# A hybrid encoder layer on one core: the first stage's order written by hand, with convolution steps between the state-space transposes, and the first two feed-forward weights split in front of the product before them

## The chip, the cores and the metric

The kernel runs on one core of one Trainium2 chip. A core has five engines with queues of their own, which meet only through semaphores: TensorE (PE in the profile; PEld is its weight load), VectorE (DVE), ScalarE (ACT), GpSimd (POOL) and SyncE (SP). [...] The metric is the device time of one execution in microseconds, as a median over runs. Lower is better.

## The reference

One encoder layer over 512 rows of width 1024, in float32. Cut to what is computed:

```python
h = rms_norm(x, norm_mix_g);  p = h @ w_in          # q|k|v (512 each) | conv input (512) | u (256)
o_sb   = stick_breaking_attention(q, k, v)          # 8 heads x 64, causal, q and k normalised
o_conv = conformer_conv(p[..., s3:s4], ...)         # gate, causal depthwise conv (31 taps), LayerNorm, swish, product
o_ssm  = s5_ssm(p[..., s4:], ...)                   # 16 groups x 16 channels, 64 complex states each
x = x + concat(rms_norm(o_sb), rms_norm(o_conv), rms_norm(o_ssm)) @ w_out
x = x + memory_cross_attention(rms_norm(x), rms_norm(mem), ...)   # 4 heads x 256, 256 memory rows
gate, up = split(rms_norm(x) @ ffn_w_in)            # hidden 2816
x = x + (silu(gate) * up) @ ffn_w_out
```

and, of the state-space branch, whose coefficients stand in the change:

```python
dt = exp(log_dt);  mag = exp(lr * dt)
ar, ai = mag * cos(li * dt), mag * sin(li * dt)
fr, fi = ((ar - 1) * lr + ai * li) / den, (ai * lr - (ar - 1) * li) / den     # den = lr*lr + li*li
bbr, bbi = fr * br - fi * bi, fr * bi + fi * br
```

## The kernel before, in words

**Products.** Each float32 operand is split into a high part (a cast to fp32r) and a low part (the rest). `mm3` (L112) makes a product of three matmuls, high x high and the two mixed ones, so L114, L115 and L116 are nearly all matmuls of the profile. A weight is loaded by `load_k` (L104) and `load_w` (L89): a DMA from SP into a staging buffer of the ring `wst` (3 buffers), a cast on ACT into `whi`, a subtraction on DVE into `wlo` (rings of 4). Where DVE is to be spared, ACT writes the negative of the high part into the low buffer, and a DMA from POOL adds the weight to it. A buffer of a ring is given out again when all that reads it is done.

**Order.** The program is written as generators. A planner places instructions on each engine by their place in the program and by when their inputs should be there; `yield` numbers tell `weave` (L187) how much PE time of side work to put in between. Inside `manual_schedule(engines=...)` the instructions of the named engines keep the order in which they are written; instructions from outside still slip in between them.

**The first stage** (L893 to L1024). The 512 rows of x come in four blocks (`squares`, `scale`, `turn`, `low`, L936 to L966: sum of squares on ACT, normalisation on DVE, 8 transposes on PE with casts on ACT, low parts on DVE). Beside it runs `ssm` (L287), the state-space branch S5, stepped by `aside` (L928) and `next(S5)`:

- L303 to L349: `dt`, the eight angles `th` (seven multiplications, L307), sine and cosine as polynomials on DVE; two Exp on ACT, `mag` and `r4` (L322, L323).
- L361 to L378: the table E on POOL, by doubling.
- L381 to L424: some 33 operations on eight columns and six on 128 (`apr`, `api`, `fr`, `fi`, `bb`) on DVE.
- L428 to L437: the product u (96 matmuls of 256 columns), copied by ACT to `uT`; L439 to L451: eight transposes of `uT` into `uk`, DVE copies, eight more into `UT`, ACT copies.
- L455 to L485: `wr`, `wi`, `Qr`, `Qi` (`products`) on DVE, and their transposes `wT`; L489 to L502: the products `kp`, copied to `Kf` on ACT, finished on DVE (L501); from L505 the products S, the scans V (L524), X, y, then the gated output and its norm (to L581).

In the block of L974 the orders of DVE, ACT and POOL are by hand, PE's isn't. It ends with the first `next(S5)` behind the E memsets, which builds E. The second `next(S5)` (L1007), from L381 through `UT`, stands outside. Then `weave` runs S5 with side work: `conv_gemm` (L584: 96 matmuls of 512 columns in eight steps, weights wc0 to wc3; its gating, L605 and L606, makes `hp`), then the attention projections `sb_proj(0)` and `sb_proj(1)` (L669), each step with three of the 62 convolution taps (L617) on DVE. The attention stage opens its memory only when S5 is done (L1018).

**The start of the feed-forward stage** (L1335 to L1373). The last cross-attention product xo has four row blocks t, each 8 x 3 matmuls of 512 columns with the weights wx10 to wx13 (`wo_rows`, L1185). Behind each block come the residual and norm (`wo_norm`, `wo_scale`), 8 transposes (`hf_turn`) and splits (`hf_split`). The FFN's first product is done by a scheme of seven half-size products (units of weights a and b, `unit_raw` L1246; sums of them `unit_tsum`, `unit_t`; sums of the rows T1 to T4). The first two units' weights a are split by `unit_a_queue` (L1266), with ACT casts into `whi` and `wlo` and an adding DMA from POOL. In this block PE, DVE, ACT and POOL all follow the written order.

Of the kernel before, what the change touches and what calls it, by code (L numbers as in the profile page):

```python
# [11 lines left out]
F32 = mybir.dt.float32  # L12
F32R = mybir.dt.float32r
# [59 lines left out]
def layer(ctx: ExitStack, tc: tile.TileContext, A: dict, out: bass.AP, dbg=None):  # L73
# [35 lines left out]
    def cols(parts, c):  # L109
        return [x[:, c] for x in parts]  # L110
# [176 lines left out]
    def ssm(sp, sk, wu):  # L287
# [17 lines left out]
        yield 0  # L305
        for k in range(1, NA):
            v.tensor_scalar(th[:, k, :], th[:, 0, :], float(LC * 2 ** (k - 1)), None, op0=ALU.mult)  # L307
            yield 0
# [12 lines left out]
        yield 0  # L321
        s.activation(mag, lrdt, AF.Exp)  # L322
        s.activation(r4, lrdt, AF.Exp, scale=float(LC))  # L323

# [23 lines left out]
        yield 0  # L348
        v.tensor_scalar(cs, x2, -2.0, 1.0, op0=ALU.mult, op1=ALU.add)  # L349
        yield 0  # L350

# [14 lines left out]
        for k in range(7):  # L366
# [10 lines left out]
            for x in {3: (wr, wi), 5: (Kf,)}.get(k, ()):  # L377
                g.memset(x, 0.0)  # L378
        yield 2

        apr = small("apr", LC + 1, NST)  # L381
# [42 lines left out]
        v.tensor_tensor(bb[:, 1], b1, b2, op=ALU.add)  # L424
        yield 0


        uT = sp.tile([P, 2, LC, NCH], F32, tag="uT", name="uT")  # L428
        pu = [ps("acc", f"u{ct}") for ct in range(2)]
        for h in range(2):  # L430
            c = slice(h * 256, h * 256 + 256)
            for ct in range(2):
                for k in range(KD):
                    o = (k % 4) * 256 + ct * P
                    mm3(pu[ct][:, c], cols(wu[k // 4], slice(o, o + P)), [x[:, k, c] for x in xn], k == 0, k == KD - 1)
        for ct in range(2):
            s.copy(uT[:, ct].rearrange("p j c -> p c j"), pu[ct].rearrange("p (c j) -> p c j", j=LC))  # L437

        uk = sp.tile([P, NST, LC, 32], F32, tag="wTr", name="uk")  # L439
        UT = sp.tile([P, NST, NCH], F32, tag="UT", name="UT")  # L440
        for ct in range(2):
            pt = ps("tp", f"uk{ct}")
            for j in range(LC):
                te.transpose(pt[:, j * P:(j + 1) * P], uT[:, ct, j, :], ident)
            v.tensor_copy(uk[:, ct * 4:ct * 4 + 4], pt.rearrange("p (j t h) -> p t j h", j=LC, h=32))
        for hf in range(2):
            pt = ps("tp", f"UT{hf}")
            for k in range(4):
                T = hf * 4 + k
                te.transpose(pt[:, k * P:(k + 1) * P], uk[:, T].rearrange("p j h -> p (j h)"), ident)  # L450
            s.copy(UT[:, hf * 4:hf * 4 + 4, :].rearrange("p t c -> p (t c)"), pt)  # L451

        yield SSM_FILL[0]
# [129 lines left out]

    def conv_gemm():  # L584
        order = (2, 0, 3, 1)
        pa = {n: ps("acc", f"cv{n}") for n in order}

        def step(n, k, b):
            o = (k % 2) * 512 + n * P
            mm3(pa[n], cols(b, slice(o, o + P)), [x[:, k, :] for x in xn], k == 0, k == KD - 1)  # L590

        for kc in range(2):
            b = load_k(A["w_cv"], 2 * kc, 512, f"wc{kc}")
            for k in (2 * kc, 2 * kc + 1):
                for n in order:
                    step(n, k, b)
                yield 2600
        b = [load_k(A["w_cv"], 2 * kc, 512, f"wc{kc}") for kc in (2, 3)]
        for n in order:
            for k in range(4, KD):  # L600
                step(n, k, b[k // 2 - 2])
            if n < 2:
                with tc.high_priority(offset=EV_CONV):
                    sg = cvp.tile([P, SEQ], F32, tag="csg", name=f"csg{n}")
                    sigmoid(sg, pa[2 + n])  # L605
                    v.tensor_tensor(hp[:, n, CPAD:], pa[n], sg, op=ALU.mult)  # L606
            yield 2600
# [285 lines left out]
    with tc.tile_pool(name="ssmp", bufs=1, side="right") as sp:  # L893
# [80 lines left out]
        with tc.manual_schedule(engines={v.engine, s.engine, g.engine}):  # L974
            for b in range(3):
                for x in vzs[b]:
                    g.memset(x[:, :, 1, :].bitcast(F32), 0.0)
            aside(18)
            squares(0)
            aside(2)  # L980
            scale(0)
            squares(1)
            turn(0)
            aside(2)
            u_high(0)
            scale(1)
            low(0)
            turn(1)
            squares(2)
            aside(99)  # L990
            g.memset(hp[:, :, :CPAD], 0.0)
            g.memset(tmpm, -2.0 ** 100)
            g.affine_select(out=tmpm, in_=tmpm, pattern=[[1, P]], compare_op=ALU.is_ge, fill=0.0, base=0, channel_multiplier=-1)
            u_low(0)
            low(1)
            u_high(1)
            squares(3)
            scale(2)
            turn(2)
            u_low(1)  # L1000
            scale(3)
            turn(3)
            low(2)
            low(3)
            next(S5)
        dbg("xn", xn)
        next(S5)  # L1007
        mxc = [slotB("mxc" + i, F32R, i, 1) for i in "hl"]
# [4 lines left out]
        T = conv_taps()  # L1013
        side = chain(conv_gemm(), along(sb_proj(0), T, 3), along(sb_proj(1), T, 3))
        weave(S5, side)
# [152 lines left out]
    with tc.tile_pool(name="ff", bufs=1, side="right") as ff:  # L1168
# [15 lines left out]

        def wo_rows(t):  # L1185
            acc = ps("acc", f"xo1{t}")
            for k in range(KD):
                mm3(acc, [x[:, k % 4, t * P:(t + 1) * P] for x in oT[k // 4]], cols(wo1[k // 2], slice((k % 2) * 512, (k % 2) * 512 + 512)),
                    k == 0, k == KD - 1)
            return acc  # L1190

# [73 lines left out]

        def unit_a_queue(p, x, a, b, w):  # L1266

            h, l = [wp.tile([P, 2, 512], F32R, tag="w" + part, bufs=WB, name=f"wa{p}{x}{part}") for part in ("hi", "lo")]
            s.copy(h, a)
            s.activation(l, h, AF.Copy, scale=-1.0)  # L1270
            g.dma_start(l.rearrange("p j n -> p (j n)"), A["w_gu"][p, x, 0], accum_op=ALU.add)  # L1271
            w["11"], w["12"] = [(h[:, i], l[:, i]) for i in range(2)]
# [63 lines left out]
        ws = {i: unit_raw(*units[i], v) for i in range(2)}  # L1336
        outs, pts = {}, {}
        with tc.manual_schedule(engines={te.engine, v.engine, s.engine, g.engine}):
            for t in range(NT):
                acc = wo_rows(t)  # L1340
                if t > 0:
                    hf_turn(t - 1)
                if t == NT - 1:
                    unit_a_queue(*units[1], *ws[1])
                wo_norm(t, acc)
                if t == NT - 1:
                    hf_diff(t - 1)
                    unit_tsum(*units[0], *ws[0], v)
                wo_scale(t)
                if t == NT - 2:  # L1350
                    unit_a_queue(*units[0], *ws[0])
                if t > 0:
                    hf_split(t - 1)
# [117 lines left out]
```

## Time and profile before

| | us |
|---|---|
| median of 3 runs | 821.97 (818.88 to 825.33) |
| profiled execution | 821.17 |
| its span in the trace | 819.5 |

The span runs from the first instruction to the last; 1.7 us of the execution lie around it. A row of a timeline has the start, the length, the engine, the line, the operation with output <- input, the shape and the count, and, in brackets, how long the engine stood idle before it and what ended that. Rows of matmuls overlap: the distance from one start to the next is the rate. "Granted clock" is the share of full speed that TensorE's clock had in a stretch.

### The profile page before, as it was taken

What the parts mean: (1) busy time and instruction counts of PE and PEld (TensorE: products, weight loads), DVE (VectorE), ACT (ScalarE), POOL (GpSimd) and SP (SyncE); (2) the same over time, 40 slices, a digit from 0 to 9 for tenths busy, and PEclk for the clock granted to TensorE, in tenths of its full rate; (3) what the DMA queues carried; (4) which work ended last, traced back from release to release, by engine and by line L of the source; (5) the groups of instructions that cost most, each with busy time, mean ns of one, the idle gap of its engine ahead of it and who ended that gap; (6) DMA issues with size and microseconds to landing.
All of it is one profiled execution on the core that took longest, in us unless ns stands there. A gap on an engine that the chain in (4) does not pass through costs nothing.

```text
span 819.5 us, 12228 instructions
## 1 busy us (share of the span) xinstructions
PE 783.1 (96%) x4640; PEld 685.2 (84%) x4640; DVE 623.6 (76%) x1079; ACT 415.4 (51%) x771; POOL 180.5 (22%) x155
## 2 busy tenths in 40 slices
PE   5799999999999999999999789999999999999998
PEld 3678999887776778888888789999999999888886
DVE  8979989677998958466847699899999997333333
ACT  6345385997878837355624654344444442322320
POOL 4910011000000000000000006676666761000000
PEclk9979999998999999999999999999999999999999
DMA  6232578525122323320451422333333322232222
GB/s 221 72 84 58 117 156 179 122 84 181 33 94 87 104 83 117 109 78 26 129 154 52 78 81 100 104 104 103 105 113 121 121 85 71 84 103 81 99 78 102
DMA packets 25116, 83.42 MB, mean 102 GB/s; under 512 B 3041, under 2 KB 3297, under 8 KB 25058
## 3 DMA queue, kind: packets, MB, share of 16 engines
q1 hardware_dynamic: 22466, 75.31, 28.9%
q0 software_dynamic: 2592, 7.34, 5.8%
q8 instruction: 36, 0.59, 0.3%
q14 instruction: 22, 0.18, 0.1%
HBM read 80.54 MB, written 2.10 MB: 101 GB/s over the span
## 4 chain that ended last, share of the span: by engine, by line
PE 83%; DVE 10%; ACT 2%; issue 2%; DMA 1%; POOL 0%; POOLq 0%; DVEq 0%
PE fo L115 5%; PE fo L114 5%; PE fo L116 5%; PE f L116 2%; PE f L115 2%; PE f L114 2%; PE qkv L114 2%; PE qkv L116 2%; PE qkv L115 2%; PE xo L114 2%; PE xo L115 2%; PE xo L116 2%; PE xq L114 2%; PE xq L116 2%; PE xq L115 2%
## 5 line engine op out<-in xcount | busy, mean ns | idle before, releaser
L617 DVE SCALAR_TENSOR_TENSOR cac<-hp,pk,cac 128x512 f32<-128x512 f32 x60 | 42.3, 742 | 0.0
L1251 POOL TENSOR_TENSOR wgb<-wgb 128x512 f32<-128x512 f32 x18 | 33.0, 1831 | 40.2 <-DMA wgb<-in_w_gu_dram 30.1
L1276 POOL TENSOR_TENSOR wga<-wga 128x512 f32<-128x512 f32 x20 | 27.3, 1363 | 41.3 <-DVE wga L1275 41.3
L1252 POOL TENSOR_TENSOR wgb<-wga,wgb 128x512 f32<-128x512 f32 x18 | 36.0, 2002 | 0.3
L1271 POOL DMA_DIRECT2D wa00lo<-in_w_gu_dram x1 | 0.9, 880 | 159.9 <-ACT wa00lo L1270 159.9
L1324 POOL TENSOR_TENSOR aF<-aF,fup 128x1024 f32<-128x1024 f32 x10 | 34.2, 3420 | 6.2 <-DVE fup L1320 5.2
L735 DVE TENSOR_TENSOR_SCAN ss<-sa,ss 128x512 f32<-128x512 f32 (+3 forms) x32 | 27.0, 859 | 2.5 <-ACT sa L731 1.9
L774 POOL TENSOR_TENSOR sqa<-sqa,sq 128x512 f32<-128x512 f32 x3 | 3.9, 1288 | 88.5 <-ACT sq L773 88.5
L1275 DVE TENSOR_TENSOR wga<-wgb,wga 128x512 f32<-128x512 f32 x22 | 22.9, 1039 | 0.0
L120 ACT CAST wTh<-wT 128x384 fp32r<-128x384 f32 (+2 forms) x40 | 14.8, 378 | 8.3 <-PE wT L750 7.0
L121 DVE TENSOR_TENSOR wTl<-wT,wTh 128x384 fp32r<-128x384 f32 (+2 forms) x40 | 16.2, 412 | 3.4 <-ACT wTh L120 3.3
L720 PE MATMUL z<-kh,qh 64*128 64x512 f32 (+3 forms) x32 | 13.2, 413 | 2.0 <-DVE ss L737 1.9
L728 ACT ACTIVATE sa<-z 128x384 f32<-128x384 f32 (+1 forms) x24 | 12.8, 532 | 4.7 <-PE z L723 4.4
L720 PEld LDWEIGHTS z<-kh,qh 64*128 64x128 f32 x32 | 6.0, 186 | 10.3 <-DVE ss L737 3.8
L737 DVE TENSOR_TENSOR ss<-z,ss 128x384 f32<-128x384 f32 (+1 forms) x24 | 14.3, 595 | 0.2
L738 ACT ACTIVATE ss<-ss 128x384 f32<-128x384 f32 (+1 forms) x24 | 13.6, 565 | 0.5 <-DVE ss L737 0.3
L730 ACT ACTIVATE sa<-sa 128x384 f32<-128x384 f32 (+1 forms) x24 | 13.8, 573 | 0.1
L731 ACT ACTIVATE sa<-sa 128x384 f32<-128x384 f32 (+1 forms) x24 | 13.7, 569 | 0.1
L750 PE MATMUL wT<-ident,ss 128*128 128x128 f32 x80 | 13.1, 284 | 0.2 <-DVE ql L124 0.2
L813 DVE SCALAR_TENSOR_TENSOR xr<-wo,rb,xr 128x512 f32<-128x512 f32 x16 | 11.9, 747 | 1.8 <-PE wo L116 1.4
L1322 ACT ACTIVATE aF<-aF 128x1024 f32<-128x1024 f32 x11 | 11.6, 1055 | 2.9 <-DVE aF L1320 1.8
L729 ACT ACTIVATE ss<-z 128x384 f32<-128x384 f32 (+1 forms) x24 | 12.8, 535 | 0.1
(2207 smaller groups left out, 3256.2 us busy)
## 6 DMA issues: line engine op xcount, KB each, us to landing
wgb<-in_w_gu_dram SPq DMA_DIRECT2D x22, 512.0 KB, 3.3
wga<-in_w_gu_dram SPq DMA_DIRECT2D x22, 512.0 KB, 3.4
for<-in_w_fo_dram SPq DMA_DIRECT2D x22, 512.0 KB, 3.3
xr<-in_x_dram SPq DMA_DIRECT2D x4, 512.0 KB, 5.0
out_dram<-xr SPq DMA_DIRECT2D x8, 256.0 KB, 2.0
xbh<-in_x_dram SPq DMA_DIRECT2D x2, 512.0 KB, 4.9
xbl<-in_x_dram SPq DMA_DIRECT2D x2, 512.0 KB, 7.7
mt<-in_mem_dram SPq DMA_DIRECT2D x2, 512.0 KB, 3.9
```

Source lines behind the costliest of these rows:

```text
L114: te.matmul(o, a[0], b[0], start=start, stop=False)
L115: te.matmul(o, a[0], b[1], start=False, stop=False)
L116: te.matmul(o, a[1], b[0], start=False, stop=stop)
L121: v.tensor_tensor(lo, src, hi, op=ALU.subtract)
L617: v.scalar_tensor_tensor(a, x, w, a, op0=ALU.mult, op1=ALU.add)
L720: te.matmul(zo, q[0], k[0], start=True, stop=False)
L735: v.tensor_tensor_scan(ts[:, c][:, ::-1], ta[:, c][:, ::-1], ts[:, c][:, ::-1], 0.0, op0=ALU.add, op1=ALU.add)
L1251: eng.tensor_tensor(b[:, 0], b[:, 1], b[:, 2], op=ALU.add)
L1252: eng.tensor_tensor(b[:, 1], a[:, 0], b[:, 1], op=ALU.subtract)
L1275: v.tensor_tensor(a[:, 0], b[:, 0], a[:, 0], op=ALU.subtract)
L1276: eng.tensor_tensor(a[:, 1], a[:, 1], a[:, 0], op=ALU.subtract)
L1324: (g if i + 1 < len(units) else v).tensor_tensor(aF[p], aF[p], dst, op=ALU.mult)
```

## The change

In the first stage:

- `th`: the seven multiplications become four, by doubling, on 1, 1, 2 and 3 columns of eight.
- the two Exp `mag` and `r4` move from in front of the polynomials to behind them.
- in `ssm`, the product u with its copies, and the transposes with theirs, move in front of the coefficients (L381 to L424), with three new yields (3, 4, 5).
- `conv_gemm` gets its weights from outside; wc0 and wc1 are loaded in the first hand-ordered block, behind the last `low`; that block now also holds u.
- a second hand-ordered block (PE, DVE, ACT) follows: twelve conv matmuls, the `uk` transposes, the load of wc2, twelve conv matmuls, the `UT` transposes, the load of wc3, two times twelve conv matmuls, the coefficients, the products with the `wT` transposes. The other half of the conv product stays side work.
- POOL's memsets of `hp` and `tmpm` and its select come first; the `aside` counts change.

At the start of the feed-forward stage:

- `wo_rows` takes a list of k: first k 0 and 1 of all four row blocks, then k 2 to 7 block by block.
- `unit_a_queue` of unit 1 comes in front of all, with its parts in a `wst` and the `fup` buffer; that of unit 0 comes between the two passes.

```diff
-        for k in range(1, NA):
-            v.tensor_scalar(th[:, k, :], th[:, 0, :], float(LC * 2 ** (k - 1)), None, op0=ALU.mult)
+        for k0, k1, c in ((1, 0, LC), (2, 1, 2), (3, 1, 4), (5, 1, 16)):
+            n = {1: 1, 2: 1, 3: 2, 5: 3}[k0]
+            v.tensor_scalar(th[:, k0:k0 + n, :], th[:, k1:k1 + n, :], float(c), None, op0=ALU.mult)
             yield 0
...
-        s.activation(mag, lrdt, AF.Exp)
-        s.activation(r4, lrdt, AF.Exp, scale=float(LC))
...
         v.tensor_scalar(cs, x2, -2.0, 1.0, op0=ALU.mult, op1=ALU.add)
+        s.activation(mag, lrdt, AF.Exp)
+        s.activation(r4, lrdt, AF.Exp, scale=float(LC))
         yield 0
...
         yield 2
 
+        uT = sp.tile([P, 2, LC, NCH], F32, tag="uT", name="uT")
...
+            s.copy(uT[:, ct].rearrange("p j c -> p c j"), pu[ct].rearrange("p (c j) -> p c j", j=LC))
+        yield 3
...
+            v.tensor_copy(uk[:, ct * 4:ct * 4 + 4], pt.rearrange("p (j t h) -> p t j h", j=LC, h=32))
+        yield 4
...
+            s.copy(UT[:, hf * 4:hf * 4 + 4, :].rearrange("p t c -> p (t c)"), pt)
+
+        yield 5
+
         apr = small("apr", LC + 1, NST)
...
         for kc in range(2):
-            b = load_k(A["w_cv"], 2 * kc, 512, f"wc{kc}")
+            b = first[kc]
...
-        b = [load_k(A["w_cv"], 2 * kc, 512, f"wc{kc}") for kc in (2, 3)]
+        b = first[2:]
...
+            g.memset(hp[:, :, :CPAD], 0.0)
+            g.memset(tmpm, -2.0 ** 100)
+            g.affine_select(out=tmpm, in_=tmpm, pattern=[[1, P]], compare_op=ALU.is_ge, fill=0.0, base=0, channel_multiplier=-1)
             aside(18)
             squares(0)
-            aside(2)
             scale(0)
             squares(1)
+            aside(6)
             turn(0)
-            aside(2)
             u_high(0)
             scale(1)
+            aside(99)
             low(0)
             turn(1)
             squares(2)
-            aside(99)
...
             low(3)
+            wc = [load_k(A["w_cv"], 2 * kc, 512, f"wc{kc}") for kc in range(2)]
             next(S5)
+            next(S5)
+        CV = conv_gemm(wc)
+        with tc.manual_schedule(engines={te.engine, v.engine, s.engine}):
+            for i in range(2):
+                next(CV)
+                next(S5)
+                wc.append(load_k(A["w_cv"], 4 + 2 * i, 512, f"wc{2 + i}"))
+            for _ in range(2):
+                next(CV)
+            for _ in range(2):
+                next(S5)
...
-        def wo_rows(t):
-            acc = ps("acc", f"xo1{t}")
-            for k in range(KD):
+        def wo_rows(t, ks):
+            if ks[0] == 0:
+                xo[t] = ps("acc", f"xo1{t}")
+            for k in ks:
...
+            if spare:
+                h = wp.tile([P, 2, 512], F32R, tag="wst", bufs=3, name=f"wa{p}{x}hi")
+                l = ff.tile([P, 2, 512], F32R, tag="fup", bufs=1, name=f"wa{p}{x}lo")
...
+            unit_a_queue(*units[1], *ws[1], spare=True)
             for t in range(NT):
-                acc = wo_rows(t)
+                wo_rows(t, (0, 1))
+            unit_a_queue(*units[0], *ws[0])
+            for t in range(NT):
+                acc = wo_rows(t, range(2, KD))
                 if t > 0:
                     hf_turn(t - 1)
-                if t == NT - 1:
-                    unit_a_queue(*units[1], *ws[1])
                 wo_norm(t, acc)
...
                 wo_scale(t)
-                if t == NT - 2:
-                    unit_a_queue(*units[0], *ws[0])
                 if t > 0:
                     hf_split(t - 1)
```

More of the change, by code (lines that the diff above doesn't have):

```diff
@@ L379, in ssm @@
         yield 2
+        uT = sp.tile([P, 2, LC, NCH], F32, tag="uT", name="uT")
+        pu = [ps("acc", f"u{ct}") for ct in range(2)]
+        for h in range(2):
+            c = slice(h * 256, h * 256 + 256)
+            for ct in range(2):
+                for k in range(KD):
+                    o = (k % 4) * 256 + ct * P
+                    mm3(pu[ct][:, c], cols(wu[k // 4], slice(o, o + P)), [x[:, k, c] for x in xn], k == 0, k == KD - 1)
+        for ct in range(2):
+            s.copy(uT[:, ct].rearrange("p j c -> p c j"), pu[ct].rearrange("p (c j) -> p c j", j=LC))
+        yield 3
+        uk = sp.tile([P, NST, LC, 32], F32, tag="wTr", name="uk")
+        UT = sp.tile([P, NST, NCH], F32, tag="UT", name="UT")
+        for ct in range(2):
+            pt = ps("tp", f"uk{ct}")
+            for j in range(LC):
+                te.transpose(pt[:, j * P:(j + 1) * P], uT[:, ct, j, :], ident)
+            v.tensor_copy(uk[:, ct * 4:ct * 4 + 4], pt.rearrange("p (j t h) -> p t j h", j=LC, h=32))
+        yield 4
+        for hf in range(2):
+            pt = ps("tp", f"UT{hf}")
+            for k in range(4):
+                T = hf * 4 + k
+                te.transpose(pt[:, k * P:(k + 1) * P], uk[:, T].rearrange("p j h -> p (j h)"), ident)
+            s.copy(UT[:, hf * 4:hf * 4 + 4, :].rearrange("p t c -> p (t c)"), pt)
+        yield 5
         apr = small("apr", LC + 1, NST)
@@ L424, in ssm @@
         v.tensor_tensor(bb[:, 1], b1, b2, op=ALU.add)
[L425 to L432, printed above, removed]
-                for k in range(KD):
[L434 to L451, printed above, removed]
         yield SSM_FILL[0]
@@ L581, in ssm, with conv_gemm @@
         branch_rstd([sqa[:, 0, :], sqa[:, 1, :]], 256, 2, sp)
-    def conv_gemm():
+    def conv_gemm(first):
         order = (2, 0, 3, 1)
@@ L989, in layer @@
             squares(2)
-            aside(99)
-            g.memset(hp[:, :, :CPAD], 0.0)
-            g.memset(tmpm, -2.0 ** 100)
-            g.affine_select(out=tmpm, in_=tmpm, pattern=[[1, P]], compare_op=ALU.is_ge, fill=0.0, base=0, channel_multiplier=-1)
             u_low(0)
@@ L1004, in layer @@
             low(3)
+            wc = [load_k(A["w_cv"], 2 * kc, 512, f"wc{kc}") for kc in range(2)]
             next(S5)
+            next(S5)
[9 more added lines that the diff above has]
+                next(S5)
         dbg("xn", xn)
-        next(S5)
         mxc = [slotB("mxc" + i, F32R, i, 1) for i in "hl"]
@@ L1013, in layer @@
         T = conv_taps()
-        side = chain(conv_gemm(), along(sb_proj(0), T, 3), along(sb_proj(1), T, 3))
+        side = chain(CV, along(sb_proj(0), T, 3), along(sb_proj(1), T, 3))
         weave(S5, side)
@@ L1183, in layer @@
         hF = {}
-        def wo_rows(t):
-            acc = ps("acc", f"xo1{t}")
-            for k in range(KD):
-                mm3(acc, [x[:, k % 4, t * P:(t + 1) * P] for x in oT[k // 4]], cols(wo1[k // 2], slice((k % 2) * 512, (k % 2) * 512 + 512)),
+        def wo_rows(t, ks):
+            if ks[0] == 0:
+                xo[t] = ps("acc", f"xo1{t}")
+            for k in ks:
+                mm3(xo[t], [x[:, k % 4, t * P:(t + 1) * P] for x in oT[k // 4]], cols(wo1[k // 2], slice((k % 2) * 512, (k % 2) * 512 + 512)),
                     k == 0, k == KD - 1)
-            return acc
+            return xo[t]
         def wo_norm(t, acc):
@@ L1264, in unit_a, with unit_a_queue @@
             w["11"], w["12"] = unit_two(p, x, "a", a, eng)
-        def unit_a_queue(p, x, a, b, w):
-            h, l = [wp.tile([P, 2, 512], F32R, tag="w" + part, bufs=WB, name=f"wa{p}{x}{part}") for part in ("hi", "lo")]
+        def unit_a_queue(p, x, a, b, w, spare=False):
+            if spare:
+                h = wp.tile([P, 2, 512], F32R, tag="wst", bufs=3, name=f"wa{p}{x}hi")
+                l = ff.tile([P, 2, 512], F32R, tag="fup", bufs=1, name=f"wa{p}{x}lo")
+            else:
+                h, l = [wp.tile([P, 2, 512], F32R, tag="w" + part, bufs=WB, name=f"wa{p}{x}{part}") for part in ("hi", "lo")]
             s.copy(h, a)
@@ L1336, in layer @@
         ws = {i: unit_raw(*units[i], v) for i in range(2)}
-        outs, pts = {}, {}
+        outs, pts, xo = {}, {}, {}
         with tc.manual_schedule(engines={te.engine, v.engine, s.engine, g.engine}):
+            unit_a_queue(*units[1], *ws[1], spare=True)
             for t in range(NT):
-                acc = wo_rows(t)
+                wo_rows(t, (0, 1))
+            unit_a_queue(*units[0], *ws[0])
+            for t in range(NT):
+                acc = wo_rows(t, range(2, KD))
                 if t > 0:
                     hf_turn(t - 1)
-                if t == NT - 1:
-                    unit_a_queue(*units[1], *ws[1])
                 wo_norm(t, acc)
```

## The prediction

> **What bounds the kernel now.** I read the page's busy shares first, then what TensorE (PE) waited for, then the table of windows, then the timeline of each engine in two places.
>
> ```profile
> span 819.5 us, 12228 instructions
> PE 783.1 (96%) x4640; PEld 685.2 (84%) x4640; DVE 623.6 (76%) x1079; ACT 415.4 (51%) x771; POOL 180.5 (22%) x155
> ```
>
> PE is the bound: 819.5 - 783.1 leaves 36.4 us that are not PE's, and only that, and matmuls run at a lower clock, can be won without removing work. PE's waits say where they are:
>
> ```profile
> PE uk L444 <- ACT uT L437: 6.4, 1, 6.4
> ...
> PE f00tp L115 <- DVE hfbl L121: 3.0, 1, 3.0
> ...
> PE f L116 <- DMA wa00lo<-in_w_gu_dram: 2.7, 1, 2.7
> ...
> PE f L116 <- DMA wa01lo<-in_w_gu_dram: 1.5, 1, 1.5
> ```
>
> The first is in the first stage (the transposes of u), the other three are at the start of the feed-forward stage (FFN). Both parts of the change aim at these four. The windows (columns: length, busy PE, PEld, DVE, ACT, POOL with counts, granted clock, DMA share, GB/s) tell what stands behind PE:
>
> ```profile
> 30.00:42.00 12.00, 5.58 (x45) 5.15 (x44) 11.48 (x27) 4.52 (x8) 11.45 (x15) 0.95 0.00 1
> 42.00:56.00 14.00, 13.26 (x56) 10.54 (x56) 13.51 (x19) 5.79 (x9) 1.67 (x4) 0.68 0.20 57
> ...
> 80.00:125.00 45.00, 43.46 (x262) 41.06 (x262) 42.19 (x72) 25.66 (x44) 6.87 (x8) 1.00 0.69 142
> 125.00:145.00 20.00, 20.00 (x111) 18.19 (x110) 19.95 (x37) 11.48 (x23) 3.45 (x4) 1.00 0.84 167
> 145.00:300.00 155.00, 149.93 (x757) 118.72 (x756) 123.62 (x253) 123.56 (x291) 6.76 (x7) 0.97 0.33 99
> ```
>
> Two things are to be seen. From 30 to 42 PE is busy 5.6 of 12 us, and from 42 to 56 its granted clock is 0.68: the wait is paid twice, 6.4 us idle and (1 - 0.68) x 14 = 4.5 us of lost speed, 10.9 us together. But VectorE (DVE) is full as well, 11.5 of 12, then 42.2 of 45 and 20 of 20. What PE wins in the first stage reaches the end only as far as DVE comes earlier too.
>
> **The first stage, part by part.** The rows on which it is worked out (DVE, POOL, ACT, PE; the kp row is of the chain of waits):
>
> ```profile
> 3.07 2.37 DVE L307 TENSOR_SCALAR th<-th 128x8 f32<-128x8 f32 x7
> ...
> 35.23 0.28 DVE L419 TENSOR_TENSOR t<-sk,fr 128x128 f32<-128x128 f32 x1
> 35.43 0.15 DVE L404 TENSOR_TENSOR ta<-ta,tb 128x8 f32<-128x8 f32 x1
> 35.62 0.17 DVE L405 TENSOR_TENSOR fi<-ta,den 128x8 f32<-128x8 f32 x1
> ...
> 39.80 1.35 DVE L466 TENSOR_TENSOR t<-bb,apr 128x384 f32<-128x384 f32 x1
> ...
> 42.39 2.29 DVE L101 TENSOR_TENSOR wc2l<-wc2s,wc2h 128x1024 fp32r<-128x1024 f32 x1
> ...
> 46.94 1.23 DVE L101 TENSOR_TENSOR wc3l<-wc3s,wc3h 128x1024 fp32r<-128x1024 f32 x1
> 48.08 0.55 DVE L466 TENSOR_TENSOR t<-bb,api 128x384 f32<-128x384 f32 x1
> ...
> 54.44 1.39 DVE L469 TENSOR_TENSOR Qi<-t,t 64x512 f32<-64x512 f32 x2
> 61.84 1.14 DVE L501 SCALAR_TENSOR_TENSOR Kf<-ident,sk,Kf 128x128 f32<-128x128 f32 x4 [6.01 <-ACT Kf L498]
> ...
> 65.22 0.69 DVE L516 TENSOR_TENSOR t<-S,E 128x512 f32<-128x512 f32 x1 [0.58 <-issue]
> ```
>
> ```profile
> 42.13 1.47 POOL L376 TENSOR_TENSOR E<-Et 128x512 f32<-128x512 f32 x1
> ```
>
> ```profile
> 40.68 1.05 ACT L437 COPY uT<-u 128x512 f32<-128x512 f32 x1
> ...
> 60.05 3.41 ACT L498 COPY Kf<-kp 32x512 f32<-32x512 f32 x8 [3.95 <-PE kp L494]
> ```
>
> ```profile
> 34.30 0.60 PE L444 MATMUL uk<-ident,uT 128*128 128x128 f32 x4
> ...
> 58.32 3.17 PE kp L494 x28
> ```
>
> u is done at 34.3, and the second uT copy came only at 40.7, behind small copies in ScalarE's (ACT's) queue. The change writes ACT's order out, the copy first, and puts twelve convolution matmuls in front of the transposes and twelve behind. So PE has work from 34.3 on: wait (6.4) and slow clock (4.5) go, -10.9 for PE.
>
> DVE pays for it. The order by hand puts the whole chain L384 to L469 behind the uk copies and two weight splits. By my count: u ends at 34.3, twelve conv matmuls of 0.23 (the spacing of two 512-wide ones in the FFN rows below) end at 37.1, eight transposes (0.45 for four) at 38.0, twelve more at 40.8, the UT transposes at 41.7, ACT's UT copy and cast of wc3 (1.05) at 43.3, DVE's split of wc3 (1.2) at 44.5. Only then the chain starts, much of which ran ahead of 36 before; DVE has nothing else to do in the gap. The chain itself: 33 small operations, 0.19 apart where one needs the last (35.43 to 35.62) and less where not, I take 0.13, 4.3 us (bounds 2.3 and 6.3); six of 0.28, 1.7; the products as in the rows from 48.08 to 55.83 (7.75) and 2.3 more for wr, 10.0. Qi ends at 60.5, where it was 55.83. The removed multiplies (seven to four at 2.37/7 = 0.34: -1.0) and the two Exp that no longer stand in front of the first Square on ACT start the rows earlier; I take 0.7 of it: +4.0 for Qi.
>
> That it is not +10 rests on one row pair: the same L466 took 1.35 while POOL built E and 0.55 once POOL was through (42.13 + 1.47), the same split 2.29 against 1.23. The late chain runs after POOL has ended.
>
> From Qi on: half of the kp products (3.17 x 16/28 = 1.8), half of the Kf casts (1.7) and the S products, an estimated 1.0, make 4.5 where it was 65.22 - 55.83 = 9.4, since kp then stood among conv matmuls. The first L516 comes at 64.3, -0.9. The four conv gating operations (about 0.6 each, 2.4), which came behind it, are done by then, and some 2.1 us of taps fit into the hole that was 6.01. DVE is ahead by 0.9 + 2.4 + 2.1 = 5.4; I take 5 (0 if gating and taps don't fit, 8 if the chain is at its lower bound).
>
> So the filled stretch to 145 ends 5 us earlier, while PE is ahead by 10.9. The remaining 6 us are then missing as fill between the attention chain's steps from 145 on. DVE and ACT are busy there 124 of 155, so the chain could run faster; I take a third, 2. First stage: -7 (bounds +6, below, and -11). Moving POOL's three small memsets, the conv loads' place in SP's queue (wc1 to wc3 wait for the same staging buffers as before) and the aside counts cost nothing: they lie beside the first loads, and without that cover they'd be some tenths.
>
> **The FFN, part by part.**
>
> ```profile
> 458.56 0.39 PE L114 MATMUL xo<-wx13h,oTh 128*128 128x512 f32 x1
> 458.79 0.39 PE L115 MATMUL xo<-wx13l,oTh 128*128 128x512 f32 x1
> ```
>
> ```profile
> 455.46 1.03 ACT L1269 CAST wa00hi<-wga 128x1024 fp32r<-128x1024 f32 x1
> ```
>
> ```profile
> 457.88 0.88 POOL L1271 DMA_DIRECT2D wa00lo<-in_w_gu_dram  x1 [159.93 <-ACT wa00lo L1270]
> ```
>
> ```profile
> 446.75 0.69 DVE L1194 TENSOR_TENSOR xr<-xo,xr 128x512 f32<-128x512 f32 x1 [0.35 <-PE xo L116]
> ...
> 449.85 1.29 DVE L1202 SCALAR_TENSOR_TENSOR hf<-xr,rny,gbf 128x1024 f32<-128x1024 f32 x1
> 451.06 1.29 DVE L121 TENSOR_TENSOR hfa<-b,hfa 128x512 fp32r<-128x512 f32 x2
> ...
> 460.44 0.68 DVE L1194 TENSOR_TENSOR xr<-xo,xr 128x512 f32<-128x512 f32 x1
> ...
> 471.30 0.69 DVE L1218 TENSOR_TENSOR t1f<-nfp,b 128x512 f32<-128x512 f32 x1 [2.99 <-PE nfp L1209]
> ...
> 478.59 1.28 DVE L121 TENSOR_TENSOR hfbl<-t3f,hfbh 128x512 fp32r<-128x512 f32 x2
> ```
>
> ```profile
> 427.33 11.21 SPq L1249 DMA_DIRECT2D wga<-in_w_gu_dram  x3
> ```
>
> ```profile
> 465.00:470.00 5.00, 3.48 (x20) 3.30 (x20) 3.31 (x6) 1.29 (x2) 0.00 (x0) 0.76 0.71 145
> ```
>
> The cast of wa00 comes at 455.5 and its adding DMA is issued at 457.9, since wx10's buffer, which it takes, was held until the last row block. With k 0 and 1 of all four blocks first, wx10 is free after 24 matmuls of 0.23 (5.5 us) instead of three blocks of 24, their transposes and six more, some 14 us earlier; wa01 uses two other buffers. Both DMAs have then ten microseconds and more before PE asks: the waits of 2.7 and 1.5 go. The price: block 0 ends 18 matmuls (4 us) later. Its norm takes 449.85 + 1.29 - 446.75 = 4.4 us, and PE has only block 1's 18 matmuls (4.1) meanwhile, so it waits some 0.5. Blocks then follow every 5.0 us on PE (18 matmuls and 0.9 of transposes) against 451.06 + 1.29 - 446.75 = 5.6 on DVE, and the last block's L1194 comes at about 461.0, not 460.4.
>
> Now what is late next. From 460.4 to 478.6 DVE works through a fixed order and idles only the 2.99 us of row 471.30, waiting for a transpose that stood behind the wa01 wait. That goes; nothing else of DVE's does. PE will still wait for hfT1l (about 3 us, 0.5 before) and for T3's hfbl (about 3, as before). So 4.2 us of waits removed turn into 2.99 + about 0.5 (the third unit's L1252 moves out of the way, since its wga now waits for a staging buffer: of the three loads in row 427.33 the third comes 30 us later, but its matmuls are 20 us off) - 0.5 = -3.0. Bounds: -1.0, if the norms slip by another microsecond and a further slow stretch comes, and -4.5, if one goes.
>
> [...] In the window from 465, behind a wait of 2.7 us, the granted clock is 0.76, so waits of 3 us will slow PE as before. [...]
>
> **Sum.** -7 - 3 = -10. The profiled execution took 821.17 us (span 819.5), 0.8 below the median 821.97: 811.2, I say 811.
>
> **Rivals.** First, PE alone counts: the taps and the attention chain follow PE, since DVE has 31 us of slack from 145 to 300. Then -10.9 and -4.5, and up to one more from the earlier rows: 805. For it: PE is busy 150 of 155 us there. Against: DVE's 20 of 20 before.
>
> Second, the first stage gives nothing: what PE wins it waits again, later, for the state-space branch, whose end opens the attention stage. Then only -3 stays: 818. For it: Qi ends 4 us later by my own count.
>
> Third, slower: DVE's stall isn't paid back. If the chain's pace in the trace is its own and not POOL's doing, it takes the 8 us more that rows such as 1.35 against 0.55 add up to; Qi ends at 68, 12 late, of which 6 fit into the old hole of 6.01: +6 - 3 + 1 for PE's wait at the wr transposes = 825. It decides from Qi at about 62 on. Against: the pairs 1.35/0.55 and 2.29/1.23. [...]
>
> Fourth, the FFN part doesn't do what it says: the casts of wa01 wait for wga01 or for wx13's buffer and the DMAs land late all the same; 814 with the first stage as forecast.
>
> **How the numbers follow.** Forecast (811, its own range 806 to 816) 0.42; PE alone 0.18; nothing from the first stage 0.22; slower 0.10; FFN without effect 0.08. One per cent is 8.2 us, about what a measurement of this kernel tells from no change, so faster means below 813.8: three quarters of the forecast, all of the first rival and half of the last, 0.53. Slower means above 830: half of the third, 0.06. The same: 0.41. The range reaches from just under the first rival (803) to no gain at all (821).
>
> **What would show it.** Right: no wait of uk on uT; granted clock near 1.00 from 42 to 56; DVE idle some 8 us between 28 and 37; L387 to L405 at below 0.2 us each after 43; Qi's end at 58 to 62; no PE wait on wa00lo or wa01lo; waits on hfT1l and hfbl of about 3 us each; no 2.99 idle on DVE at L1218. Wrong: Qi after 64, PE idle again between 100 and 145, or the attention stage as long as before with PE less busy in it.

## The result, and the profile after

| | before | after |
|---|---|---|
| median of 12 runs, us | 821.07 | 815.52 |
| lowest to highest, us | 818.73 to 825.33 | 812.91 to 818.20 |
| profiled execution, us | 821.17 | 816.98 |
| its span, us | 819.5 | 815.3 |

The ratio is 0.9927 (95% interval 0.9911 to 0.9942): 0.7% faster, 5.6 us. By the bound of 1% that is "the same". The forecast was 811, its range 803 to 821.

PE's waits after, the longest first (those of the first 25 us left out):

```profile
PE f00tp L115 <- DVE hfbl L121: 3.0, 1, 3.0
...
PE o L114 <- ACT wTh L120: 1.9, 1, 1.9
PE z L723 <- DVE ss L740: 1.8, 4, 1.0
PE f00z L114 <- ACT hfT1h L120: 1.7, 1, 1.7
...
PE f00z L115 <- DVE hfT1l L121: 0.7, 1, 0.7
```

Three of the four waits that the change aimed at are gone (uk, wa00lo, wa01lo). A new one has come inside the attention stage (o); the one on z is as long as before (1.8 us, it was 1.9). Three windows after, in stretches of the table before:

```profile
30.00:42.00 12.00, 12.00 (x75) 10.63 (x75) 4.71 (x4) 5.21 (x7) 11.61 (x11) 1.00 0.36 102
42.00:56.00 14.00, 12.95 (x63) 10.38 (x62) 12.88 (x51) 8.48 (x20) 2.07 (x5) 1.00 0.65 149
...
145.00:300.00 155.00, 146.45 (x719) 113.59 (x718) 126.65 (x256) 119.16 (x278) 5.92 (x6) 0.94 0.30 92
```

PE got what it was promised: from 30 to 42 it is busy 12.00 of 12 us where it had 5.58, and from 42 to 56 its clock is 1.00 where it was 0.68. It gave most of it back later: from 145 to 300 it is busy 146.5 us instead of 149.9, at 0.94 instead of 0.97. Where the lead dies is read from three PE rows of each kernel: the first matmul of the third block of projections, the first matmul of the attention scores z, and the last (not shown). Before, then after:

```profile
128.81 0.33 PE L114 MATMUL qkv<-ws20h,xnh 128*128 128x384 f32 x1
...
141.83 0.49 PE L720 MATMUL z<-kh,qh 64*128 64x512 f32 x1
```

```profile
119.27 0.52 PE L114 MATMUL qkv<-ws20h,xnh 128*128 128x384 f32 x1
...
139.07 0.51 PE L723 MATMUL z<-kh,qh 64*128 64x512 f32 x2
```

PE reaches the projections 9.5 us earlier, and the first z only 2.8. The last matmul into z starts at 278.50 before and at 276.11 after, so the 2.4 us that are left at the end of the stage are those of its start. What held the first z is on DVE: the scores need the normalised q and k (qk), which the attention front (`sb_front`) makes there. Before, then after:

```profile
124.59 0.16 DVE L284 COPY rb<-br2y 128x4 f32<-128x4 f32 x1
...
138.48 1.22 DVE L694 TENSOR_TENSOR qk<-qk,rqy 128x1024 f32<-128x1024 f32 x1
...
144.41 0.74 DVE L617 SCALAR_TENSOR_TENSOR cac<-hp,pk,cac 128x512 f32<-128x512 f32 x1
```

```profile
121.54 0.29 DVE L121 TENSOR_TENSOR vzl<-qkv,vzh 128x128 fp32r<-128x128 f32 x1 [1.67 <-ACT vzh L120]
...
126.72 0.16 DVE L284 COPY rb<-br2y 128x4 f32<-128x4 f32 x1
...
134.41 1.22 DVE L697 TENSOR_TENSOR qk<-qk,rqy 128x1024 f32<-128x1024 f32 x1
...
146.98 0.74 DVE L620 SCALAR_TENSOR_TENSOR cac<-hp,pk,cac 128x512 f32<-128x512 f32 x1
```

The end of the state-space branch (rb) comes 2.1 us later than before, and so does the last of the 62 convolution taps (L617, now L620), by 2.6. In between, the small operations of two norms stand one by one behind taps of 0.74 us, and qk comes 4.1 us earlier where PE comes 9.5. So DVE was not 5 us ahead at 145: with its taps it was behind.

### The profile page after: what moved, and what is told of

It reads as the page before. It is cut to its first block, busy times and chain, and to the rows that moved or that the text cites. A ratio compares the mean times of both kernels' runs of the same rounds, so it can differ in the third digit from the quotient of the medians.

```text
span 815.3 us, 12237 instructions
## 1 busy us (share of the span) xinstructions
PE 783.3 (96%) x4640; PEld 685.1 (84%) x4640; DVE 618.2 (76%) x1076; ACT 416.7 (51%) x771; POOL 180.3 (22%) x155
## 4 chain that ended last, share of the span: by engine, by line
PE 78%; DVE 14%; ACT 4%; issue 1%; DMA 0%; POOL 0%; DVEq 0%; POOLq 0%; ACTq 0%
PE fo L115 5%; PE fo L116 5%; PE fo L114 5%; PE f L115 2%; PE f L114 2%; PE f L116 2%; PE xq L114 2%; PE xq L116 2%; PE xq L115 2%; PE xo L114 2%; PE xo L116 2%; PE xo L115 2%; PE qkv L115 2%; PE qkv L116 2%; PE qkv L114 2%
## 5 line engine op out<-in xcount | busy, mean ns | idle before, releaser
L620 DVE SCALAR_TENSOR_TENSOR cac<-hp,pk,cac 128x512 f32<-128x512 f32 x60 | 43.0, 743 | 0.2
L114 PE MATMUL o<-wTh,vzh 128*128 128x512 f32 (+3 forms) x32 | 11.7, 366 | 1.9 <-ACT wTh L120 1.9
```

Of the source, the lines that this page charges most:

```text
L114: te.matmul(o, a[0], b[0], start=start, stop=False)
L620: v.scalar_tensor_tensor(a, x, w, a, op0=ALU.mult, op1=ALU.add)
```

## The experiments

The two theories at the start: the attention stage is a chain with a start of its own, and PE's lead is lost because the start does not move (C); or PE sets the stage and loses the lead by waits and clock (D). All times below are ratios to runs of the kernel before on the same chip, from 4 to 12 runs of each kernel but e11 (e3 has 5, e7 has 4); the experiments ran on three chips, so rows are compared by their ratios. The columns on the right are PE rows as above, "last z" being the last matmul into z (the expectations count to the first matmul of its group, 1.3 us earlier).

| run | ratio | 95% interval | ws20h | first z | last z | first to last |
|---|---|---|---|---|---|---|
| before | 1 | | 128.81 | 141.83 | 278.50 | 136.7 |
| the change | 0.9927 | 0.9911 to 0.9942 | 119.27 | 139.07 | 276.11 | 137.0 |
| e1 FFN part only | 0.9942 | 0.9921 to 0.9963 | 126.72 | 139.74 | 276.19 | 136.5 |
| e2 first stage only | 0.9957 | 0.9934 to 0.9979 | 118.61 | 137.33 | 274.06 | 136.7 |
| e3 change, front ahead | 0.9807 | 0.9779 to 0.9835 | 118.56 | 130.00 | 266.14 | 136.1 |
| e4 before, front ahead | 0.9967 | 0.9947 to 0.9987 | 125.97 | 136.69 | 272.77 | 136.1 |
| e5 change, chain early | 0.9930 | 0.9907 to 0.9954 | 124.90 | 144.90 | 277.37 | 132.5 |
| e6 e3, chain early | 0.9911 | 0.9885 to 0.9938 | 125.22 | 138.18 | 275.42 | 137.2 |
| e7 change, less PE work | 0.9884 | 0.9853 to 0.9915 | 119.07 | 138.78 | 274.94 | 136.2 |
| e8 before, less PE work | 1.0012 | 0.9990 to 1.0034 | 128.13 | 141.14 | 278.10 | 137.0 |
| e9 change, pool only | 0.9921 | 0.9898 to 0.9945 | 119.31 | 139.13 | 276.14 | 137.0 |
| e10 change, one pass | 0.9971 | 0.9955 to 0.9987 | 119.01 | 137.73 | 276.04 | 138.3 |
| e11 change, seven th | one run, 815.15 us | | 119.01 | 137.73 | 276.39 | 138.7 |
| e12 e3, whole chain ahead | 1.0024 | 1.0004 to 1.0044 | 118.70 | 128.55 | 283.11 | 154.6 |

One caution for all rows: before, e1 and e8 have the same program up to 230 us, and their first z lie at 139.74 to 141.83, the end of the branch (rb) at 120.94 to 124.59. In the change and the five others with its order there (e2, e7, e9, e10, e11) the two lie at 137.33 to 139.13 and at 126.03 to 126.72. So a single profile tells the first z to about 2 us and the branch's end to 4, and the two groups do not overlap.

**The two parts alone (e1, e2).** e1 is the kernel before with the diff's hunks in `wo_rows`, `unit_a_queue` and the FFN's order; e2 is it with all the others.

> The kernel before with the feed-forward part of the change alone. Theory A (the two parts are independent, and the first stage gives what the residual additions at the border show, 432.70 to 430.28, so 2.4 us): this part gives -3.0 at the split of hfbl, as forecast, and -2 to -3 at the end, about 818.5. Rival B (the first stage's gain is larger and is lost again in the feed-forward stage): this part alone gives nothing or less than 1 us.

> The kernel before with the first-stage part of the change alone. Theory A: -2 to -3 us, about 818.5, with the border of the feed-forward stage at 430.3 and the first z at 139.1, as in the whole change. Rival B: -5 or more at the end, since the stages behind keep the gain when the feed-forward part does not take it.

The FFN part gives 0.6%, 4.8 us, the first stage 0.4%, 3.5 us; together 8.3 against the 6.0 of 0.9927, which the intervals allow. Theory A holds in its form (two independent parts); it had both parts smaller, and its -2 to -3 lies at the edge of the first interval and inside the second. Rival B is out.

**The attention front ahead of the taps (e3, e4, e9).** The same edit on both kernels; e9 has only the pool of its first line.

```diff
-        branch_rstd([sqa[:, 0, :], sqa[:, 1, :]], 256, 2, sp)
+        with tc.high_priority(offset=EV_SB): branch_rstd([sqa[:, 0, :], sqa[:, 1, :]], 256, 2, cvp)
...
-        fronts = {0: sb_front(0, pr[0][0], sbp)}
+        with tc.high_priority(offset=EV_SB): fronts = {0: sb_front(0, pr[0][0], sbp)}
```

> The changed kernel, with the end of the state-space branch (the four small operations of the branch norm, whose tiles move to another pool, so that the attention pool opens at the bss matmuls) and the first attention front put ahead of the convolution taps in DVE's queue; nothing else is reordered by hand. Theory C (the attention stage is a chain of its own length: 141.83 to 277.21 us from the first to the last z before, 139.07 to 274.83 after, 135.4 and 135.8, and it starts when the front comes out of DVE): the first z comes 4 to 8 us earlier and the end follows by most of it, so -4 to -7 against the changed kernel, 809 to 812. Rival D (PE sets the stage; its lead was lost by the granted clock and by the planner's order): the first z comes earlier, the last does not, -1 to +1. Rival E (DVE sets it: the taps that are pushed back cost later what the front wins): -1 to +1 with DVE's waits moved behind the taps.

> The same edit on the kernel before, in which PE has no lead when the attention stage starts (the third block of projections begins at 128.8 instead of 119.3). Theory C in its plain form: the same gain as in the changed kernel, -4 to -7. Theory C with PE close behind the chain (150 of 155 us busy there before): less, -1 to -4, so that edit and change together give more than each by itself. Rivals D and E: -1 to +1.

> The changed kernel with one half of the third experiment alone: the branch norm's tiles move to another pool, so that the attention pool opens at the bss matmuls, and no priority is given. Theory H (the opening of the pool holds the front): most of the -10 us of the third experiment, first z at 131 to 134. Theory I (the front is held by its place among the taps in DVE's queue; the pool only by the 1 to 2 us between two taps): first z 1 to 2 us earlier, 137 to 138, and the time -1 to -2 against the changed kernel.

e3 runs at 807.05 us, 15.6 below the kernel before and by the ratios (0.9807 to 0.9927) 1.2% below the change; it beats both kernels. The first z comes 9.1 us earlier, more than expected, the last z 10.0: the end follows the start. DVE in e3:

```profile
124.80 1.22 DVE L697 TENSOR_TENSOR qk<-qk,rqy 128x1024 f32<-128x1024 f32 x1
```

The normalisation of q and k stands at 124.8 instead of 134.4. The taps it passes end two microseconds later (the last at 148.92) and cost nothing: rival E is out. On the kernel before, the same edit gives 2.7 us. There q and k are normalised as early as in e3, but PE begins its third block of projections only at 125.97, and the first z comes 10.7 us after that (11.4 in e3): the scores stand behind projections that PE has not done yet. DVE in e4:

```profile
123.84 1.22 DVE L694 TENSOR_TENSOR qk<-qk,rqy 128x1024 f32<-128x1024 f32 x1
```

So each of the two, PE's lead and the front's place, is worth little without the other: 3.5 us for the first stage, 2.7 for the front, and together 11 (e3's 1.93% are 15.8 us, less the 4.8 of the FFN). By the intervals, the front's edit is worth 1.1 to 4.4 us on the kernel before and, an estimate from those of e3 and the change, 7 to 13 on the changed one. e9 shows that the pool's opening was not what held the front: nothing moved, against both H and I, which had expected at least 1 us. It is the place among the taps. The edit raises two things, the branch norm (rb comes at 122.21 instead of 126.72) and the front; they were not tried apart.

**Less PE work inside the attention stage (e7, e8).** In the key projection from memory, the product of the high and the low part is left out (32 matmuls):

```diff
-            mm3(acc[t][:, :n], a(k, t), ...)
+            (mm2 if name.startswith("xa_wk") else mm3)(acc[t][:, :n], a(k, t), ...)
```

> The changed kernel without the third of the three products (high part by low part) of the key projection from memory (32 of 96 matmuls of 0.23 us, 7.4 us of PE left out, all between 231 and 282 us, inside the attention stage). Theory C (a chain of its own length): first to last z stays at 136 to 137 us, PE is busy some 7 us less in it, and the end moves by 0 to -2. Rival D (PE sets the stage): the length falls by 5 to 7 us.

> The same left out of the kernel before. Theory C: 136 to 137 us from first to last z here too, and the end at 0 to -2. Theory C with PE close behind the chain, as the edit on the front suggested: 134 to 136, -1 to -3. Rival D: -5 to -7, and more than in the changed kernel, where PE has a lead.

The windows of e7, then of e8:

```profile
145.00:300.00 155.00, 145.36 (x694) 112.78 (x693) 127.12 (x260) 119.00 (x278) 6.97 (x6) 0.91 0.30 94
```

```profile
145.00:300.00 155.00, 146.95 (x723) 116.59 (x722) 123.80 (x255) 122.28 (x292) 7.22 (x7) 0.93 0.33 99
```

The lengths stay at 136.2 and 137.0 us; the PE work left out turns into idle time and a lower clock (0.91 where it was 0.94, 0.93 where it was 0.97). The kernel before gains nothing (+0.1%), the changed one 0.4%, about 3.5 us, more than the 0 to 2 that C had, though an estimate from the two intervals reaches from 0.7 to 6.4. PE is busy 150 of 155 us, and yet less work for it did not make its stage shorter: D's 5 to 7 us are out. PE's clock is another matter, as e5 shows next.

**The small operations moved ahead of uk (e5, e6).** The block L415 to L455 goes from behind `yield 5` to the line ahead of `yield 3`, so that DVE fills its empty stretch with it.

> The changed kernel, with the chain of small operations L415 to L436 and the six for bb put ahead of the two uk copies, into DVE's empty stretch from 31 us; its operations then run beside POOL again. The products end earlier by the forecast's own count: the chain of 5.1 us and the six of 1.7 leave the stretch behind the wc3 split, so Qi ends at 55 to 58 instead of 63.9. Theory F (the start of the attention stage hangs on the state-space branch, and that on Qi): the first z comes 4 to 6 us earlier and the end with it, 810. Rival G (Qi is not what the branch waits for; the front's place among the taps decides): the first z moves by less than 2 us and the time by -1 to +1 against the changed kernel.

> The same chain of small operations moved, on the kernel of the third experiment, in which the attention front stands ahead of the taps. Theory F: the first z 4 to 6 us earlier than there (130.0), and 802. Rival G: the branch's end and the front as there, 806 to 808.

DVE after, where the block runs once POOL is through, then e5, where it runs beside POOL:

```profile
36.44 1.29 DVE L401 COPY uk<-uk 128x512 f32<-128x512 f32 x2 [5.03 <-PE uk L400]
...
43.25 0.16 DVE L415 TENSOR_TENSOR apr<-mag,cs 128x8 f32<-128x8 f32 x1
...
48.23 0.17 DVE L436 TENSOR_TENSOR fi<-ta,den 128x8 f32<-128x8 f32 x1
...
52.29 0.69 DVE L155 SCALAR_TENSOR_TENSOR csg<-cv,csg 128x512 f32<-128x512 f32 x1
...
62.55 1.38 DVE L472 TENSOR_TENSOR Qi<-t,t 64x512 f32<-64x512 f32 x2
...
64.63 0.68 DVE L520 TENSOR_TENSOR t<-S,E 128x512 f32<-128x512 f32 x1
```

```profile
31.08 0.57 DVE L396 TENSOR_TENSOR apr<-mag,cs 128x8 f32<-128x8 f32 x1
...
33.18 0.16 DVE L403 TENSOR_TENSOR tb<-api,apr 128x8 f32<-128x8 f32 x1
...
36.09 1.26 DVE L400 TENSOR_TENSOR tb<-api 128x8 f32<-128x8 f32 x1
...
42.51 0.17 DVE L417 TENSOR_TENSOR fi<-ta,den 128x8 f32<-128x8 f32 x1
...
44.18 1.28 DVE L445 COPY uk<-uk 128x512 f32<-128x512 f32 x2
...
58.27 1.39 DVE L472 TENSOR_TENSOR Qi<-t,t 64x512 f32<-64x512 f32 x2
```

The same 33 operations take 5.1 us (43.25 to 48.23 and the last one) and 11.6 (31.08 to 42.51 and the last one). Qi ends 4.3 us earlier, less than expected, since the chain is slower there; and the uk copies come 7.7 later, and PE's wait is back at the next step:

```profile
PE UT L451 <- DVE uk L445: 5.9, 1, 5.9
```

```profile
42.00:56.00 14.00, 11.08 (x49) 9.26 (x49) 11.56 (x26) 7.80 (x18) 1.15 (x2) 0.76 0.50 119
```

The third block of projections comes 5.6 us later than in the change, the first z 5.8. Theory F falls, and so does G as it was put: the first z moved, the other way. e5 ends level with the change all the same (0.9930), with 132.5 us from first to last z, the one run that is shorter. Both profiles have the same 636 matmuls in this stretch (the rows count a few at its edges too). The change, then e5:

```profile
139.07:276.11 137.04, 130.96 (x638) 100.84 (x637) 117.80 (x228) 112.59 (x256) 5.51 (x6) 0.94 0.32 95
```

```profile
144.90:277.37 132.47, 125.89 (x637) 97.13 (x637) 114.69 (x225) 112.68 (x256) 6.12 (x6) 0.97 0.32 98
```

PE is idle 6.1 us of the one and 6.6 of the other, so the 4.6 us are those of the clock, 0.94 against 0.97. e10 and e11, with the same matmuls again, take 138.3 and 138.7 us at 0.93. So of rival D this much stands: with the same work, the stage is longer where PE's clock is lower. Why the clock falls less in e5 is not known. In e6 the lost lead shows in the time: 0.9911 instead of 0.9807.

**The FFN in one pass (e10).** The second unit's early split and its own buffers stay, `wo_rows` goes back to one pass, and the first unit's split to its place behind the third row block:

```diff
-            for t in range(NT):
-                wo_rows(t, (0, 1))
-            unit_a_queue(*units[0], *ws[0])
...
-                acc = wo_rows(t, range(2, KD))
+                acc = wo_rows(t, range(KD))
```

> The changed kernel with the second unit's weight split early in its own two buffers as in the change, but the output product in one pass over its eight k as before, and the first unit's split behind the third row block as before. Theory J (the forecast's account: PE's waits of 2.7 us on wa00lo and 1.5 us on wa01lo hold the nfp transposes, and DVE idles 2.99 us for them): the wait on wa00lo is back, the one on wa01lo stays away, DVE idles about 1.5 us at L1234, and from the first residual addition at the border (L1176) to the split of T3's hfbl it takes 44 to 44.8 us, between 42.9 in the changed kernel and 45.9 before; the time +1 to +2 against the changed kernel. Rival K (the early split of the second unit is all that counts): 42.9, no difference. Rival L (the two passes are all that counts): 45.9, +3.

PE's waits and DVE's rows of e10:

```profile
PE f00tp L115 <- DVE hfbl L121: 4.9, 1, 4.9
...
PE f L116 <- DMA wa00lo<-in_w_gu_dram: 2.7, 1, 2.7
```

```profile
432.27 1.28 DVE L1176 TENSOR_TENSOR xr<-xo,xr 128x512 f32<-128x512 f32 x2
...
468.00 0.68 DVE L1234 TENSOR_TENSOR t1f<-nfp,b 128x512 f32<-128x512 f32 x1
...
473.36 0.69 DVE L1268 TENSOR_TENSOR wgb<-wga,wgb 128x512 f32<-128x512 f32 x1 [1.74 <-DMA wga<-in_w_gu_dram]
...
477.11 1.28 DVE L121 TENSOR_TENSOR hfbl<-t3f,hfbh 128x512 fp32r<-128x512 f32 x2
```

From the border (the first residual addition, L1176) to hfbl it takes 44.8 us, in between, as J said; the time is 0.4% worse than the change's, 3.6 us, more than J's 1 to 2, though an estimate from the two intervals reaches from 1.8 to 5.4. K, with no difference, is out; L has the time, but not the 45.9. J's way is not seen: DVE does not idle at L1234, where J had 1.5 us. But this profile cannot settle it, since behind the wait of 2.7 us on wa00lo PE's clock stayed at 1.00, where it fell to 0.50 in the kernel before. The kernel before, then e10:

```profile
464.00:467.00 3.00, 3.00 (x16) 3.00 (x16) 2.98 (x4) 2.29 (x4) 0.00 (x0) 0.50 1.02 223
```

```profile
464.00:467.00 3.00, 3.00 (x27) 3.00 (x26) 3.00 (x5) 1.76 (x3) 0.00 (x0) 1.00 0.33 134
```

With the clock of before, PE would come some 1.5 us later in e10 (an estimate: half of these 3 us), as much as J had. In the kernel before, the wait on wa01lo took that up: in e4, where the clock stayed at 1.00 too, this wait is 3.1 us instead of 1.5. What does cost in e10 is the load of the third unit, which is issued 37.5 us after the border (35.3 in the change) and holds DVE for 1.74 us. So the two passes of the change save that, beside the wait on wa00lo.

**The angles (e11).** The seven independent multiplications stand in the place of the four.

> The changed kernel with the seven independent multiplications of th by constants in the place of the four dependent ones. The forecast counted the four as 1.0 us cheaper. Theory M (a dependent one pays the latency of the one ahead of it: 3.19 us for four, 2.37 for seven): the group takes 2.4 us again and the DVE work behind it, the scaling of the second row block (L950, at 12.4 to 12.6), comes 0.3 to 0.8 us earlier; the end within the run to run spread. Rival: POOL's memsets beside them make the difference, and the seven take 3 us or more too.

The group in the changed kernel, then in e11:

```profile
2.98 3.19 DVE L308 TENSOR_SCALAR th<-th 128x8 f32<-128x8 f32 x4
```

```profile
3.01 2.80 DVE L307 TENSOR_SCALAR th<-th 128x8 f32<-128x8 f32 x7
```

Seven take 2.80 here and took 2.37 before: half of the loss comes with the four, half with what stands beside them now (POOL's two small memsets and its select moved ahead are a possible cause, not tried alone). Neither M (2.4) nor its rival (3 or more) is met. The scaling of the second row block comes at 11.81 instead of 12.60. The end is not told apart from the run to run spread.

**The whole attention chain ahead (e12).** To e3, the priority of each group of weights is added:

```diff
-                pend.append((p, gi, sb_weights(p, gi, fronts[p], sbp)))
+                with tc.high_priority(offset=EV_SB): pend.append((p, gi, sb_weights(p, gi, fronts[p], sbp)))
```

> The kernel of the third experiment with the same priority also for every group of attention weights (scores, Abs to Exp, scan), so that they stand ahead of taps, evictions and splits in the queues. Theory C in its full form (the length of 136 us from first to last z is the chain's latency through queues shared with side work): the length falls to 125 to 132 and the time by 3 to 8 us, to about 800. Rival N (the chain's length is its own engines' time and the side work is what remains at the end): first to last z shorter by as much as the projections and the memory keys behind it come later; the time -1 to +2.

It costs 2.2% against e3. The first z comes at 128.55, the last at 283.11, and PE is busy only 140.79 of the 155 us from 145. The stage is 18 us longer, where C in its full form and N both had it shorter; both fall. So the 136 us are no property of the chain alone; they go with this interleaving. What sets them step by step stays open.

## Why the prediction was right or wrong

The number was 4.5 us too low, inside the range; the first stage gave half of what it was to give. Step by step:

- *PE wins 10.9 us in the first stage.* Right in kind: no wait of uk, 12.00 of 12 us, clock 1.00. PE is 9.5 us ahead at the third block of projections. But the 10.9 was the price in one profile: in e1, with the same program there, the wait is 3.7 us and the clock from 42 to 56 is 0.88, in e8 6.9 and 0.73, and against e1 PE is ahead by 7.5.
- *DVE's late chain starts at 44.5 and takes 4.3 + 1.7 us, Qi ends at 60.5 - 0.7.* It started at 43.25 and took 5.1 + 1.7, but Qi ended at 63.9. Row 52.29 shows why: the gating and the first taps, which were to come behind Qi, slipped in between the products. The order by hand does not keep others out.
- *The first L516 at 64.3.* Right in number (row 64.63; L516 is L520 now), but by luck: Qi ended 4.1 us later than forecast, and the 4.5 us behind it were 0.7, since the Kf operations, which came ahead of it before, came behind it:

```profile
67.61 1.14 DVE L504 SCALAR_TENSOR_TENSOR Kf<-ident,sk,Kf 128x128 f32<-128x128 f32 x4
```

- *DVE is 5.4 us ahead at 145, take 5.* This is the step that failed. Four gating operations and four taps were done by the first L520, as said, but the eight Kf operations (2 x 1.14 us), done before it in the kernel before, were not, so by an estimate some 3 us of lead were left of the 5.4. DVE then waited on ACT and PE in its order (1.67 us at 121.54), and the last tap ended 2.6 us later than before. The forecast carried a lead across 80 us in which DVE serves other engines, without asking what starts the next stage.
- *A third of PE's other 6 us counts in the attention stage.* The size was off: none of it shows there. The stage is as long as before (137.0 and 136.7 us), and work left out does not shorten it (e7, e8). The first stage measured -3.5 (e2) for -7. Its bounds held.
- *The multiplications save 1.0 us.* Wrong sign: they cost 0.8 in the profiles (3.19 against 2.37).
- *FFN -3.0.* Right by its own count: hfbl comes 42.90 us after the border where it came 45.89, with both waits and the 2.99 us of idle time gone. The rows after, and the border row before:

```profile
430.28 1.28 DVE L1176 TENSOR_TENSOR xr<-xo,xr 128x512 f32<-128x512 f32 x2
...
473.18 1.29 DVE L121 TENSOR_TENSOR hfbl<-t3f,hfbh 128x512 fp32r<-128x512 f32 x2
```

```profile
432.70 1.28 DVE L1161 TENSOR_TENSOR xr<-xo,xr 128x512 f32<-128x512 f32 x2
```

The time says 4.8 (3.0 to 6.5). The waits on hfT1 came as foretold (1.7 + 0.7 us, about 3 said), that on hfbl too.

Of the rivals, "PE alone counts" is out by the time (805 said) and by e8. "The first stage gives nothing" had the right place, the opening of the attention stage, and the wrong holder: not the pool that opens at the branch's end (e9), but the front's place among the taps. "Slower" is out: e5 shows that the slow rows of the chain were POOL's doing (11.6 us beside it, 5.1 once it was through). The point from which it was to decide was wrong too: Qi ended behind 62, and the first L520 was still in time. The FFN did what it said. Of the three signs named for a wrong forecast, one came true: the attention stage as long as before, with PE less busy in it. Of those for a right one, two failed: Qi's end (63.9, not 58 to 62) and DVE's empty stretch (5.0 us at row 36.44, not 8). In the chances, half of 0.10 was put at 0.06; it is 0.05.

## What to carry to other kernels

A lead of the busiest engine is worth something only if the next stage's start comes earlier too (here PE was 9.5 us ahead and the first z 2.8): find the instruction that opens the stage and the queue that it stands in. A busy share of 97% (150 of 155 us) does not say that less work for an engine makes its stage shorter (136.2 and 137.0 us with 32 matmuls left out, 137.0 and 136.7 with them); leave out some of it and see, and compare the granted clock, which can lengthen the same work (the same 636 matmuls took 137.0 us at 0.94 and 132.5 at 0.97). Two edits that gave 3.5 and 2.7 us alone were worth 11 together, since each removed what hid the other, so an edit with a small result is tried again once the next wait is gone.

## What the runs showed of the hardware

**TENSOR_TENSOR operations of DVE beside POOL.** In e5 those of 0.16 us take up to 1.26 (row 36.09) while POOL runs TENSOR_TENSOR operations of its own, and 0.16 to 0.17 again from 33.09 to 33.93, beside a MEMSET on POOL:

```profile
32.97 0.96 POOL L379 MEMSET Kf<- 128x1024 f32 x1
33.89 1.04 POOL L372 TENSOR_TENSOR Et<-E,cs 128x512 f32<-128x512 f32 x1
```

The whole chain took 5.1 us once POOL was through (the change) and 11.6 beside it (e5). No row of it has a wait on POOL before it: the operations themselves are longer, so here the two engines met otherwise than through semaphores. How, the traces do not show.

**The clock after short waits.** The FFN is the same program in the changed kernel and in e11. After:

```profile
473.00:476.00 3.00, 1.48 (x7) 1.48 (x8) 3.00 (x6) 3.00 (x6) 0.00 (x0) 0.61 0.34 135
476.00:479.00 3.00, 3.00 (x16) 3.00 (x16) 2.67 (x5) 0.35 (x1) 0.00 (x0) 0.50 0.02 5
```

In e11:

```profile
467.00:470.00 3.00, 1.79 (x7) 1.60 (x8) 3.00 (x5) 2.20 (x5) 0.00 (x0) 0.74 0.75 264
470.00:473.00 3.00, 3.00 (x20) 2.94 (x18) 2.97 (x6) 1.63 (x4) 0.00 (x0) 0.69 0.35 104
```

After, the slow stretch follows the wait of 3.0 us on hfbl and is paid in full: PE is busy all of the 12 us from 476 to 488, at 0.50 and 0.75 of its clock up to 482 and at 1.00 behind that. In e11 it follows waits of 1.7 and 0.7 us, lies ahead of the wait on hfbl, and shortens it to 1.6: it costs almost nothing (an estimate: the two windows lost 0.26 x 1.79 + 0.31 x 3.00 = 1.4 us of speed, and the wait is 1.4 us shorter). The forecast, from the window from 465, had waits of 3 us slow PE, and in the profiled run of the change that held. It is no rule: behind the same wait of 2.7 us on wa00lo the clock fell to 0.50 in the kernel before and stayed at 1.00 in e10, as the windows from 464 to 467 show. What decides it, no run shows.
